# The place of three plain units in the first pair of each feed-forward stage, and of a set of constants

## The chip, the cores and the metric

The kernel runs on one core of a Trainium2 chip (trn2). The metric is device time of one execution in microseconds (us), the median of several runs. The engines named below are PE (matrix products), ACT (ScalarE), DVE (VectorE), POOL (GpSimd) and SP, which only issues transfers.

## The reference, cut to what matters

One decoder layer on 256 tokens of width 2048 in float32: a half-step feed-forward stage (width 5632), a mixer with two attention branches, and a second feed-forward stage, each with a residual and a layer norm. What the change touches:

```python
def _swiglu(x, w_gate, w_up, w_down):
    return (jax.nn.silu(x @ w_gate) * (x @ w_up)) @ w_down

# in the mixer, from the positions and four small vectors
cos, sin = jnp.cos(ang), jnp.sin(ang)
s = s - slopes[None, :, None, None, None] * dist[:, None, None, :, :]
s = jnp.where(_causal_mask(q0, q1), s, -jnp.inf)
lam = (jnp.exp(jnp.sum(lq1.astype(f32) * lk1.astype(f32)))
       - jnp.exp(jnp.sum(lq2.astype(f32) * lk2.astype(f32))) + lambda_init)
```

## The kernel before

**Products.** Every float32 factor is split in two parts: a rounded high part (L154, a cast on ACT) and the rest (L155, a subtraction on DVE). `triple` multiplies high by high, high by low and low by high: the three matmuls of L208, L209 and L210, 128x512 each. Split weights lie in a ring of pairs, `wring`; in gate and up there are six (`set_ring(6)`), so a weight block can be split only when the unit that used its pair last has run on PE. An even wring number is a pair's high part, the odd one behind it the low part.

**Units.** Work is queued in units. Each has a load (a DMA that SP issues), a `prep` (the split) and a `now` (its matmuls). `look(3, 4)` keeps three units loaded and four prepared ahead of the one that runs. Tile's scheduler then orders what each engine does, within the dependences and some `issue_after` constraints. Loads go out in SP's order: `raw` tiles of plain units (L482, 4 buffers, one is free when DVE has subtracted from it), and the seven-product blocks `sraw` and `eraw` (L443).

**The gate and up products** of a feed-forward stage work on pairs of column groups of the weights, w0 and w1. `Hybrid` computes most of the inner dimension by seven block products in place of eight (products 1 to 7), and the rest by plain units: `p` on w0, `q` on w1, 12 matmuls each. A product has three units: two with 6 matmuls, from `sraw` blocks of 128x1024, and a third with 3, from an `eraw` block of 128x512; 15 matmuls. The string in ORDERS gives the order; "n" stands where product 1 of the next pair goes. The key is (wide, seeded). All pairs of both feed-forward stages are wide; the first pair of each stage is not seeded (`p > 1` in the call), so (True, False) serves these two pairs alone. Feed-forward 1 runs from the start, feed-forward 2 behind the mixer; they are called stage 1 and stage 2 here.

**What the products read.** Product 1 uses block "11" of w0. When it has been split, a DMA on POOL that adds to its target (L458) puts block "12" of w1 on top of it; product 5 uses that sum. Product 3 uses block "22" as it is. For product 6, DVE adds the sum in "11" to "22" (L451); then POOL adds "12" to it by DMA (L453) for product 7. Products 1, 6 and 7 sum up in bank X, products 5 and 3 in bank Z, whose tile is called `tr`; the other banks' tiles are called `mm`. Behind product 5 ACT copies bank Z away (L409, in `after`), before product 3 writes it; behind products 1, 6 and 7 it copies bank X (L408).

**The constants of the mixer** (`setup`, L1099 to L1154: the mask, the biases of the attention, sines and cosines, lambda) are made during `down` of stage 1. `later(70, setup)` runs its code when 70 more units have run; from there on the scheduler places its instructions, most of them small ones on DVE.

Of the kernel before, what the change touches and what calls it, by code (L numbers as in the profile page):

```python
# [59 lines left out]
def layer_kernel(ctx: ExitStack, tc: tile.TileContext, a: dict, out: bass.AP):  # L60
# [42 lines left out]
    def later(n, fn):  # L103
        uid[0] += 1
        heapq.heappush(todo, (step[0] + n, uid[0], fn))
# [209 lines left out]
    class Extra:  # L315
# [7 lines left out]
        def make(self):  # L323
# [12 lines left out]
            for b, p in enumerate((2, 4)):  # L336
# [4 lines left out]
            V.scalar_tensor_tensor(out=lo, in0=a0, scalar=-1.0, in1=hi.bitcast(F32), op0=ALU.mult, op1=ALU.subtract)  # L341
            self.at_[1] = [hi, lo]

    ORDERS = {(False, False): "1pp5p36np27q4qqq", (True, False): "1p5p36np27q4qq",
              (False, True): "1pp5p36np27q4qqq", (True, True): "1p5p36np27q4qq"}
    WIDE = 5
    line = []
# [8 lines left out]
    class Hybrid:  # L356
# [35 lines left out]
        def group(self, w0, w1, done, wide=False, seeded=False, gates=False):  # L392
# [115 lines left out]
            else:  # L508
                order = ORDERS[wide, seeded]
            turn = {n: iter(range(WIDE if wide else 4, end + 1)) for n in range(2)}  # L510
# [421 lines left out]
    def ffn(n, x, wgu, wdn, residual, g, bt, each, first=None, between=None, nxt=None, cols=None, norm=None, pending=None):  # L932
# [100 lines left out]
                       ((24, 26, 48, 50) if pending is None else (13, 14, 60, 62), (94, 97, 100, 103)),  # L1033
                       35 if cols is None else None, pending, () if pending is None else (17, 32, 67, 82))
        if n == 1:
            later(70, setup)
        spare = []
        forms = {q: QuadForms(spare) for q in range(3)}
        down = Sliced(h_at)
# [462 lines left out]

    h1 = Acts(KD, "h1", (0, 1))
    ffn(1, xq, a["gu1"], a["dn1"], a["x"], a["ln1_g"], a["ln1_b"], keep(0), first_tokens, second_tokens, h1, a["ln1_cols"])

    yq = mixer(h1)
# [4 lines left out]
    for c in range(4):  # L1511
        project(a["w_out"][c], yq, KD, 512, lambda b, bank, c=c: ln.evac(c, b, bank),
                hook=at_unit(0, widen) if c == 3 else None)
    catch_up(0)

    ffn(2, h2, a["gu2"], a["dn2"], res[1], a["ln3_g"], a["ln3_b"],
        lambda b, c, z, o=slice(0, 512): (nc.scalar if o.start else nc.sync).dma_start(
            out[b * P:(b + 1) * P, c * 512 + o.start:c * 512 + o.stop], z), norm=ln,
# [66 lines left out]
def _build(arrays):  # L1585
    import numpy as np
    import concourse.bacc as bacc

    nc = bacc.Bacc("TRN2", target_bir_lowering=False, num_devices=1)
    aps = {k: nc.dram_tensor(f"in_{k}_dram", v.shape, mybir.dt.from_np(v.dtype), kind="ExternalInput").ap()  # L1590
           for k, v in arrays.items()}
    out = nc.dram_tensor("out_0_dram", (T, D), F32, kind="ExternalOutput").ap()
    with tile.TileContext(nc) as tc:
        layer_kernel(tc, aps, out)
    return nc
# [9 lines left out]
```

## Time and profile before

| | us |
|---|---|
| median of 3 runs | 1982.29 |
| lowest, highest run | 1978.77, 1983.79 |
| profiled execution, its own time | 1982.59 |
| its span | 1980.8 |
| PE busy in it | 1960.7 |
| mean granted clock of PE (1 is full) | 0.996 |

A row of the timeline gives start and duration in us, engine, line, operation, what is written and read, shapes, and in brackets how long the engine stood idle before it and what released it. Rows of POOLq and SPq are the issue of a transfer; its data lands later. A matmul's duration is the time through the array; a new one starts each 0.23 us. PE is idle where a start comes later than that.

### The profile page before, as it was taken

Reading aid. Unit: us, or ns where it says so; the run is one execution under the profiler, and the core shown is the slowest. Engines: PE = TensorE matmul, PEld = TensorE weight load, DVE = VectorE, ACT = ScalarE, POOL = GpSimd, SP = SyncE. Lnnn points to the kernel's source line nnn. Section 1 sums busy time; section 2 is a strip of 40 time slices with the busy share of each in tenths; the row PEclk is TensorE's granted clock in tenths of the full one; section 3 lists DMA queues with packets and bytes.
Section 4 is the critical chain, followed back from the end, with each engine's and each line's share of the span. In section 5 each row is a group of like instructions: output and inputs, shape, how many; then the busy total and the mean of one; then the engine's idle time right before and its main releaser. Section 6 shows DMA issues by size and latency. Waiting matters only on the chain. (4 is left out here: it accounts for less than half of the span.)

```text
span 1980.8 us, 25910 instructions
## 1 busy us (share of the span) xinstructions
PE 1960.7 (99%) x8751; PEld 1617.2 (82%) x8751; DVE 1743.7 (88%) x2161; ACT 1269.4 (64%) x1660; POOL 367.8 (19%) x600
## 2 busy tenths in 40 slices
PE   9899999999999999999999999999999999999998
PEld 8788888888878888888888888887888888888886
DVE  7799999999898879999987777779999999999997
ACT  6567766676656576666667655556767667766662
POOL 0112221222100010102241530011222123210000
PEclk9999999999999999999999999999999999999999
DMA  8888888787867657668686798688888878887773
GB/s 308 257 258 227 248 276 275 223 257 258 302 211 247 196 187 296 232 213 255 214 255 202 228 303 275 204 274 246 235 252 284 265 221 245 264 323 242 275 233 125
DMA packets 151958, 489.93 MB, mean 247 GB/s; under 512 B 21984, under 2 KB 22288, under 8 KB 151824
## 3 DMA queue, kind: packets, MB, share of 16 engines
q1 hardware_dynamic: 111744, 374.78, 53.4%
q0 software_dynamic: 39936, 113.35, 24.0%
q8 instruction: 68, 1.11, 0.2%
q14 instruction: 66, 0.54, 0.1%
q10 hardware_dynamic: 144, 0.13, 0.0%
HBM read 457.77 MB, written 30.41 MB: 246 GB/s over the span
## 5 line engine op out<-in xcount | busy, mean ns | idle before, releaser
L154 ACT CAST wring<-raw 128x1024 fp32r<-128x1024 f32 (+2 forms) x460 | 474.1, 1035 | 298.9 <-PE mm L210 211.7
L155 DVE TENSOR_TENSOR wring<-raw,wring 128x1024 fp32r<-128x1024 f32 (+2 forms) x460 | 545.4, 1198 | 111.0 <-ACT wring L154 108.7
L154 ACT CAST wring<-sraw 128x1024 fp32r<-128x1024 f32 x436 | 456.2, 1052 | 175.7 <-PE mm L210 67.4
L155 DVE TENSOR_TENSOR wring<-sraw,wring 128x1024 fp32r<-128x1024 f32 x436 | 524.5, 1217 | 47.8 <-ACT wring L154 43.7
L208 PE MATMUL mm<-wring,h 128*128 128x512 f32 (+2 forms) x1176 | 454.4, 386 | 0.0
L209 PE MATMUL mm<-wring,h 128*128 128x512 f32 (+2 forms) x1176 | 452.4, 385 | 0.4 <-DVE wring L155 0.4
L210 PE MATMUL mm<-wring,h 128*128 128x512 f32 (+2 forms) x1176 | 452.6, 385 | 0.0
L208 PEld LDWEIGHTS mm<-wring,h 128*128 128x128 f32 x1176 | 221.2, 188 | 47.0 <-ACT snap L409 3.3
L209 PEld LDWEIGHTS mm<-wring,h 128*128 128x128 f32 x1176 | 221.1, 188 | 44.1 <-DVE wring L155 1.1
L210 PEld LDWEIGHTS mm<-wring,h 128*128 128x128 f32 x1176 | 221.1, 188 | 43.8 <-DVE h L155 0.9
L209 PE MATMUL mm<-wring,xs 128*128 128x512 f32 x616 | 239.9, 390 | 0.2 <-DVE wring L155 0.2
L208 PE MATMUL mm<-wring,xs 128*128 128x512 f32 x616 | 240.1, 390 | 0.0
L210 PE MATMUL mm<-wring,xs 128*128 128x512 f32 x616 | 239.7, 389 | 0.0
L451 DVE TENSOR_TENSOR sraw<-sraw,sraw 128x1024 f32<-128x1024 f32 x128 | 153.7, 1217 | 1.2 <-DMA sraw<-in_wgm_dram 0.7
L209 PEld LDWEIGHTS mm<-wring,xs 128*128 128x128 f32 x616 | 115.7, 188 | 25.1 <-DVE wring L155 1.0
L210 PEld LDWEIGHTS mm<-wring,xs 128*128 128x128 f32 x616 | 115.6, 188 | 24.1
L208 PEld LDWEIGHTS mm<-wring,xs 128*128 128x128 f32 x616 | 115.6, 188 | 24.1
L749 POOL DMA_DIRECT2D hT<-blocks x176 | 98.4, 575 | 182.5 <-DVE blocks L747 94.8
L453 POOL DMA_DIRECT2D sraw<-in_gu_dram x40 | 35.1, 885 | 435.4 <-DVE sraw L451 410.5
L208 PE MATMUL mm<-wring,x 128*128 128x512 f32 x264 | 103.8, 396 | 0.4 <-ACT wring L154 0.4
L209 PE MATMUL mm<-wring,x 128*128 128x512 f32 x264 | 103.4, 392 | 0.2 <-DVE wring L155 0.2
L210 PE MATMUL mm<-wring,x 128*128 128x512 f32 x264 | 103.3, 391 | 0.0
(350 smaller groups left out, 2876.7 us busy)
## 6 DMA issues: line engine op xcount, KB each, us to landing
raw<-in_gu_dram SPq DMA_DIRECT2D x150, 512.0 KB, 6.3
raw<-in_dn_dram SPq DMA_DIRECT2D x140, 512.0 KB, 4.6
sraw<-in_gu_dram SPq DMA_DIRECT2D x120, 512.0 KB, 6.7
sraw<-in_gu_dram POOLq DMA_DIRECT2D x80, 512.0 KB, 7.0
sraw<-in_dn_dram SPq DMA_DIRECT2D x36, 512.0 KB, 5.7
raw<-in_w_out_dram SPq DMA_DIRECT2D x32, 512.0 KB, 4.4
eraw<-in_gu_dram SPq DMA_DIRECT2D x60, 256.0 KB, 6.9
hraw<-hT POOLq DMA_DIRECT2D x56, 256.0 KB, 5.1
```

The source lines that it names most:

```text
L154: cast[0] = S.copy(hi, src)
L155: lows[0] = V.tensor_tensor(out=lo, in0=src, in1=hi.bitcast(F32), op=ALU.subtract)
L208: PE.matmul(o, xh, wh, start=first, stop=False, skip_group_check=again)
L209: PE.matmul(o, xh, wl, start=False, stop=False, skip_group_check=again)
L210: PE.matmul(o, xl, wh, start=False, stop=last, skip_group_check=again)
L451: last = V.tensor_tensor(out=R[src][i], in0=R[src][i], in1=R[add[1]][i], op=ALU.add)
L453: nc.gpsimd.dma_start(R["22"][s], source("12", s), accum_op=ALU.add)
L749: nc.gpsimd.dma_start(to.rearrange("(g r) (i f) -> i r g f", g=4, i=4)[i], t[32 * i:32 * (i + 1), :].rearrange("r (g f) -> r g f", g=4))
```

## The change

```diff
--- before.py
+++ after.py
@@ -341,7 +341,7 @@
             V.scalar_tensor_tensor(out=lo, in0=a0, scalar=-1.0, in1=hi.bitcast(F32), op0=ALU.mult, op1=ALU.subtract)
             self.at_[1] = [hi, lo]
 
-    ORDERS = {(False, False): "1pp5p36np27q4qqq", (True, False): "1p5p36np27q4qq",
+    ORDERS = {(False, False): "1pp5p36np27q4qqq", (True, False): "1ppp536n27q4qq",
               (False, True): "1pp5p36np27q4qqq", (True, True): "1p5p36np27q4qq"}
     WIDE = 5
     line = []
@@ -1033,7 +1033,7 @@
                        ((24, 26, 48, 50) if pending is None else (13, 14, 60, 62), (94, 97, 100, 103)),
                        35 if cols is None else None, pending, () if pending is None else (17, 32, 67, 82))
         if n == 1:
-            later(70, setup)
+            later(84, setup)
         spare = []
         forms = {q: QuadForms(spare) for q in range(3)}
         down = Sliced(h_at)
```

The string keeps its three p, three q and all products. Before, one plain unit stood between products 1 and 5, one between 5 and 3, and one between the next pair's product 1 and product 2. In the new string all three stand between products 1 and 5: none between 5 and 3, and none between the next pair's product 1 and product 2. The second edit runs the code of `setup` 14 units later. Every engine has as many instructions as before.

Product 5 to product 3 on PE, stage 1. `xe` is the activations' side of a product's third unit, `xs` that of the first two, `x` that of a plain unit. Before, from the third unit of product 5 on:

```order
L208 MATMUL tr_546<-wring_120,xe_261 128x512
L209 MATMUL tr_546<-wring_121,xe_261 128x512
L210 MATMUL tr_546<-wring_120,xe_261 128x512
L208 MATMUL mm_530<-wring_118,x_215 128x512
L209 MATMUL mm_530<-wring_119,x_215 128x512
L210 MATMUL mm_530<-wring_118,x_216 128x512
```

After, the same third unit and what follows it:

```order
L208 MATMUL tr_576<-wring_116,xe_261 128x512
L209 MATMUL tr_576<-wring_117,xe_261 128x512
L210 MATMUL tr_576<-wring_116,xe_261 128x512
L208 MATMUL mm_497<-wring_120,xs_331 128x512
L208 MATMUL tr_576<-wring_114,xs_373 128x512
L209 MATMUL tr_576<-wring_115,xs_373 128x512
L210 MATMUL tr_576<-wring_114,xs_374 128x512
```

Before, a plain unit (`x`) follows product 5. After, the first matmul of product 6 (on `mm`) stands there, and behind it product 3 writes the bank that product 5 used.

The same stretch on ACT. Before, from the first cast of product 5 (`sraw_463`) to the copy of its bank; `sraw_465`, `sraw_466` and the second `eraw_471` are product 3's blocks:

```order
L154 CAST wring_104<-sraw_463 128x1024
L154 CAST wring_120<-eraw_471 128x512
L944 ACTIVATE sg_508<-mm_324 128x256
L154 CAST wring_102<-sraw_464 128x1024
L154 CAST wring_118<-raw_491 128x1024
L408 COPY snap_474<-mm_495 128x512
L154 CAST wring_116<-sraw_465 128x1024
L154 CAST wring_114<-sraw_466 128x1024
L154 CAST wring_104<-eraw_471 128x512
L409 COPY snap_474<-tr_546 128x512
```

After, from the first cast of product 5 to the copy of its bank:

```order
L154 CAST wring_120<-sraw_463 128x1024
L944 ACTIVATE sg_510<-mm_324 128x256
L154 CAST wring_102<-raw_488 128x1024
L154 CAST wring_118<-sraw_464 128x1024
L408 COPY snap_474<-mm_497 128x512
L154 CAST wring_116<-eraw_471 128x512
L154 CAST wring_114<-sraw_465 128x1024
L154 CAST wring_104<-sraw_466 128x1024
L154 CAST wring_102<-eraw_471 128x512
L154 CAST wring_120<-sraw_463 128x1024
L154 CAST wring_118<-sraw_464 128x1024
L409 COPY snap_474<-tr_576 128x512
```

Product 5's third block (the first `eraw_471`) is now cast behind its second (`sraw_464`), where it was ahead of it. Product 3's blocks take the ring pairs 114, 104 and 102, of which 104 and 102 were the second and third plain units' (`raw_483`, `raw_488`), and both casts of product 6 (`sraw_463` and `sraw_464` for the second time) stand ahead of the copy L409.

The loads that SP issues there. Before, from the plain unit ahead of product 3's blocks:

```order
L482 DMA raw_491<-in_gu_dram 128x1024
L443 DMA sraw_465<-in_gu_dram 128x1024
L443 DMA sraw_466<-in_gu_dram 128x1024
L443 DMA eraw_471<-in_gu_dram 128x512
L482 DMA raw_606<-in_gu_dram 128x1024
L482 DMA raw_677<-in_gu_dram 128x1024
L482 DMA raw_720<-in_gu_dram 128x1024
```

After, from the second plain unit on:

```order
L482 DMA raw_483<-in_gu_dram 128x1024
L482 DMA raw_488<-in_gu_dram 128x1024
L443 DMA sraw_465<-in_gu_dram 128x1024
L443 DMA eraw_471<-in_gu_dram 128x512
L482 DMA raw_684<-in_gu_dram 128x1024
L482 DMA raw_720<-in_gu_dram 128x1024
L482 DMA raw_731<-in_gu_dram 128x1024
L443 DMA sraw_466<-in_gu_dram 128x1024
```

Product 3's second block, `sraw_466`, is issued behind five plain loads in place of one, three of them behind its first block.

The mixer's constants on DVE, in `down` of stage 1. Before, in the middle of `setup`:

```order
L1134 TENSOR_SCALAR turns_4628<-turns_4628 128x128
L1144 TENSOR_TENSOR lp_4654<-lv_4652 128x256
L155 TENSOR_TENSOR wring_115<-raw_4497,wring_114 128x1024
L1136 SCALAR_TENSOR_TENSOR ang_4623<-turns_4628,ang_4623 128x128
L155 TENSOR_TENSOR wring_105<-sraw_3474,wring_104 128x1024
L1136 SCALAR_TENSOR_TENSOR ang_4623<-turns_4628,ang_4623 128x128
L1146 TENSOR_REDUCE ls_4656<-lp_4654 128x2
```

After, the rows at the same numbers:

```order
L1134 TENSOR_SCALAR turns_4832<-turns_4832 128x128
L1144 TENSOR_TENSOR lp_4858<-lv_4856 128x256
L155 TENSOR_TENSOR wring_115<-raw_4497,wring_114 128x1024
L155 TENSOR_TENSOR h_4782<-hraw_4699,h_4781 128x512
L155 TENSOR_TENSOR wring_105<-sraw_3474,wring_104 128x1024
L155 TENSOR_TENSOR h_4782<-hraw_4699,h_4781 128x512
L1136 SCALAR_TENSOR_TENSOR ang_4827<-turns_4832,ang_4827 128x128
```

The rows of `setup` up to here stand where they stood. From here on the L1136 rows come some places later; two subtractions of L155 for `h` go ahead.

## The prediction

> **What bounds the kernel now.** The page's busy times and the list of what PE waits for come first, then one undisturbed stretch by windows (columns: stretch, its length, busy time of PE, PEld, DVE, ACT and POOL, granted clock, DMA share, GB/s).
>
> ```profile
> PE 1960.7 (99%) x8751; PEld 1617.2 (82%) x8751; DVE 1743.7 (88%) x2161; ACT 1269.4 (64%) x1660; POOL 367.8 (19%) x600
> PE tr L208 <- ACT wring L154: 4.7, 2, 4.3
> PE tr L899 <- ACT pair L897: 4.1, 1, 4.1
> PE tr L209 <- DVE wring L155: 3.3, 3, 1.8
> 100.00:150.00 50.00, 50.00 (x221) 41.15 (x221) 46.45 (x55) 33.35 (x43) 9.56 (x14) 1.00 0.81 248
> ```
>
> PE is busy 99% of the span, and 221 matmuls fill 50 us: 0.226 us a step. No matmul goes or comes, so only the time in which PE stands still, or runs at a low clock, can change. The largest wait for a ring pair, 4.3 us on a `tr` tile, is product 5 of the first stage's first pair: where the diff works. Its PE rows (start, duration, what it waited for), from the last matmul of 5's first unit on, and the windows there:
>
> ```profile
> 57.72 0.39 PE L210 MATMUL tr<-wring,xs 128*128 128x512 f32 x1
> 62.38 0.51 PE L208 MATMUL tr<-wring,xs 128*128 128x512 f32 x1 [4.27 <-ACT wring L154]
> 63.64 0.79 PE L209 MATMUL tr<-wring,xs 128*128 128x512 f32 x1 [0.76 <-DVE wring L155]
> ...
> 69.78 0.43 PE L208 MATMUL mm<-wring,x 128*128 128x512 f32 x1
> 70.04 0.40 PE L209 MATMUL mm<-wring,x 128*128 128x512 f32 x1
> 62.40:69.80 7.40, 6.64 (x16) 4.97 (x17) 7.40 (x8) 4.74 (x7) 0.00 (x0) 0.54 0.34 117
> ```
>
> From 57.72 to 70.04 PE makes 17 steps, 3.85 us at 0.2267. They took 12.32: **8.47 us lost**. The clock row gives the shares: (1 − 0.54) × 7.40 = 3.4 us went to the low clock that followed, 5.1 to waiting. Why 5 was late, on ACT and POOL:
>
> ```profile
> 54.05 1.05 ACT L154 CAST wring<-sraw 128x1024 fp32r<-128x1024 f32 x1 [5.73 <-PE mm L210]
> 60.49 0.62 ACT L154 CAST wring<-eraw 128x512 fp32r<-128x512 f32 x1 [5.38 <-DMA eraw<-in_gu_dram]
> 61.29 1.03 ACT L154 CAST wring<-sraw 128x1024 fp32r<-128x1024 f32 x1
> 45.99 1.16 POOL L458 DMA_DIRECT2D eraw<-in_gu_dram  x1
> ```
>
> 5's third unit is cast at 60.49, when its accumulating DMA (issued at 45.99) has landed. 5's second unit stands behind it in ACT's order, so PE waited for a short tile that it needed last. Stage 2, the same place:
>
> ```profile
> 1339.99 0.39 PE L210 MATMUL tr<-wring,xs 128*128 128x512 f32 x1
> 1340.81 0.49 PE L208 MATMUL tr<-wring,xs 128*128 128x512 f32 x1 [0.43 <-ACT wring L154]
> 1342.06 0.50 PE L209 MATMUL tr<-wring,xs 128*128 128x512 f32 x1 [0.76 <-DVE wring L155]
> 1342.63 0.40 PE L208 MATMUL tr<-wring,xs 128*128 128x512 f32 x1
> 1339.98:1342.63 2.65, 1.46 (x5) 0.67 (x4) 2.14 (x4) 2.65 (x4) 0.00 (x0) 1.00 0.20 76
> 1350.13 0.39 PE L208 MATMUL mm<-wring,xs 128*128 128x512 f32 x1
> 1350.68 0.50 PE L209 MATMUL mm<-wring,xs 128*128 128x512 f32 x1 [0.17 <-DVE wring L155]
> ```
>
> 1339.99 to 1342.63 is 4 steps, 0.91 us, in 2.64: 1.74 us lost, at full clock. Product 6 starts 0.55 − 0.23 = 0.3 us late, and some 0.1 more in its next steps: 0.44.
>
> **What the change removes.** With three plains (12 matmuls, 2.72 us each) ahead of it, 5 starts 5.44 us later, at 62.0 instead of 56.6. Its second unit landed at about 57.8 (the second of the three accumulates) and now is cast ahead of the third unit, and the third is wanted only at 64.75 against a cast done near 61.1. All of 8.47 goes, in stage 2 all of 1.74 and, since 6 is delayed anyway, the 0.44. **−10.65 us.**
>
> **What it adds.** Nothing stands any more between 5 and 3 on PE. The plain that stood there gave the other engines 2.72 us for the copy of 5's bank (L409) and the splits of 3 and 6. Two things are now late, both in the orders shown above: one matmul of 6 stands ahead of 3 on PE, and ACT has L409, which must read bank Z before 3 writes it, behind 6's two casts. Durations, from the same chain in stage 2:
>
> ```profile
> 1343.98 0.62 ACT L154 CAST wring<-eraw 128x512 fp32r<-128x512 f32 x1
> 1345.94 0.68 DVE L155 TENSOR_TENSOR wring<-eraw,wring 128x512 fp32r<-128x512 f32 x1
> 1346.54 2.35 DVE L451 TENSOR_TENSOR sraw<-sraw,sraw 128x1024 f32<-128x1024 f32 x2
> 1347.84 2.14 ACT L154 CAST wring<-sraw 128x1024 fp32r<-128x1024 f32 x2 [2.75 <-DVE sraw L451]
> 1344.50 0.59 ACT L409 COPY snap<-tr 128x512 f32<-128x512 f32 x1
> ```
>
> 3's third unit takes the ring pair that the third plain frees (wring_102 in the rows of ACT), so its cast cannot start before 5 starts on PE; call that moment 0. Then: 0.2 + 0.62 the cast, 0.7 its low part, 1.2 the first add of L451, 1.1 the cast of 6: the single matmul of 6 runs at 3.9. With the steps by themselves, the add ends at 2.76; behind it follow both casts of 6 and the copy, 2.14 + 0.59: 3 may start at 5.5. 5's 15 matmuls end at 3.40 and the single one takes 0.23, so 3 should have started at 3.6: **1.9, with the restart 2.0 us lost**. This is the value for stage 2.
>
> In stage 1 the third unit of 5, which stands ahead of 3's casts in ACT's order, lands at 60.4 as before (I assume that the DMA queues are as full). 60.5 + 0.6 + 1.05 + 1.0 + 0.6: 3's casts end at 63.5; two more low parts on DVE and the add end at 66.2; 6's casts at 67.4 and 68.4, the copy at 69.0. 5 and the single matmul would have allowed 65.66: **3.1 to 3.3 us lost**; I take 3.1. If that DMA lands 1.5 us earlier, it is 2.0 as in stage 2.
>
> Does the clock drop? PE would stand from 65.4 to 67.4, then from 67.6 to 69.0. Rows of before, at the change's other place, with a similar gap:
>
> ```profile
> 589.76 0.51 PE L208 MATMUL tr<-wring,xs 128*128 128x512 f32 x1
> 592.09 0.80 PE L209 MATMUL tr<-wring,xs 128*128 128x512 f32 x1 [1.82 <-DVE wring L155]
> 589.31:595.82 6.51, 4.63 (x12) 3.17 (x11) 6.51 (x8) 3.51 (x5) 0.00 (x0) 0.74 0.64 196
> ```
>
> There 2.3 us between two starts were enough: (1 − 0.74) × 6.51 = 1.7 us lost to the clock. Stage 2's 1.74 us drew none (clock 1.00). The new gap in stage 1, 3.3 us with one matmul in it, is nearer to 590's: I add **1.7** for stage 1, nothing for stage 2; the bounds are 0 and the 3.4 of 62.40.
>
> [...]
>
> **The setup, 14 units later.** The order shows the same DVE rows in the same places up to row 612; only the short L1136 rows and what follows move by a few. The stall at 592.09 (DVE late with a low part) lies where DVE, still behind with the setup's work, is busy throughout:
>
> ```profile
> 565.55 1.02 DVE L1118 SCALAR_TENSOR_TENSOR bias<-dist,mask 128x384 f32<-128x384 f32 x2
> 572.83 1.02 DVE L1118 SCALAR_TENSOR_TENSOR bias<-dist,mask 128x384 f32<-128x384 f32 x2
> 595.36 0.22 DVE L1134 TENSOR_SCALAR turns<-turns 128x128 f32<-128x128 f32 x1
> ```
>
> The L1118 rows have not moved, so this edit costs nothing that I can see: **0**. Bounds: −4.0, if the stall went (2.3 us between starts and the clock's 1.7), and +0.4, if the setup ended late enough to hold up one more split (the 0.4 of the smallest waits on the list).
>
> **Sum.** 1982.59 (span 1980.8 and 1.8 around it) − 10.65 + 3.1 + 1.7 + 2.0 + 0 = **1978.7 us**. The profiled run lies 0.3 above the median of 1982.29, so I leave it. Measurements of this kernel can tell about 0.3% from no change, 5.9 us here: this gain of 0.2% counts as the same.
>
> **Rivals.**
> B, the same waits without a drop of the clock: 1977.0, or 1975.9 when the third unit also lands early. For it: the 1.74 us of stage 2 drew none. Against: 590 did.
> C, nothing takes the place of the stall, because the tile scheduler's order leaves more room than my chain: 1982.59 − 10.65 = 1971.9. Against: the ring pair of the third plain is a dependence, whatever the engines do.
> D, the setup does what a later place says, and the stall at 592 goes: 1978.7 − 4.0 = 1974.7. Against: the rows stand where they stood.
> E, **slower**: 3's second block (sraw_466 in SP's rows) is now issued behind three plain loads, and the last of them waits for a buffer. Loads there took:
>
> ```profile
> 39.93 7.96 SPq L482 DMA_DIRECT2D raw<-in_gu_dram  x3
> raw<-in_gu_dram SPq DMA_DIRECT2D x1, 512.0 KB, 9.7
> DMA to landing us min/median/max: 11.3/13.0/14.2
> ```
>
> The buffer is that of the second plain (raw_483), which lands 9.7 after 39.93, and is split 2.3 later: 51.9, so sraw_466 is issued near 52.2 instead of 48.5. With 7 us it lands at 59.2, hidden. With M its landing, the two splits, the add, 6's casts and the copy put 3 at M + 7.0: it decides from M = 62, and the gain is gone at about M = 64, 11.7 us after issue. The loads issued from 47.99 to 50.68 took 11.3 to 14.2. At 14.2, M = 66.4, 3 starts at 73.4, 7.7 late, with 3.4 for two slow windows: 1982.59 − 10.65 + 11.1 + 2.0 = **1985.0**. Against: those loads stood with six issued together and three accumulates; the load at 52.2 has fewer beside it.
>
> **How the numbers follow.** Forecast 0.50 (its own range 1977.8 to 1980.4: the low end with the wait at 2.2, the high end with a second slow window), B 0.28, C 0.07, D 0.06, E 0.09. The range leaves out C, the early end of D, and E beyond a small loss: 1974.3 to 1982.3. Faster by over 0.3% is below 1976.4: C, D and half of B, 0.26. Slower by over 0.3% is above 1988.2: the worst of E, 0.03. The same: 0.71.
>
> **What would show it.** In the changed kernel's profile: no wait of PE from 57.7 to 62; waits of about 2 and 1.4 us at the single matmul of 6 (for ACT's cast) and at 3's first (for L409), at about 65.4 and 67.6, and a lower clock behind them; some 2 us at the same two places in stage 2, at full clock; the wait near 590 as before. A wait of 3's second unit for its DMA means E; a stall at 590 that is gone means D. The forecast is wrong in its main step if the two new waits sum to under 1 us or over 5 in stage 1.

## The result and the profile after

| | before | after |
|---|---|---|
| median of 9 runs each, us | 1980.39 | 1976.14 |
| profiled execution, its own time | 1982.59 | 1975.02 |
| its span | 1980.8 | 1973.2 |

The ratio of after to before is 0.9974, with a 95% interval of 0.9964 to 0.9985. The forecast was 1978.7, no difference that this measurement tells from none (0.3%), in a range of 1974.3 to 1982.3. The measured gain of 0.26% is of that size, and the whole interval lies below 1. One of the nine runs after (2446.8 us, at a mean granted clock of 0.752) and one of the eight of the string-only kernel below (10628.98 us) were disturbed and are left out of the ratios.

Busy times of the changed kernel and, from the list of what its PE waits for, the three lines that bear on the change:

```profile
PE 1956.0 (99%) x8751; PEld 1614.6 (82%) x8751; DVE 1744.1 (88%) x2161; ACT 1269.9 (64%) x1660; POOL 367.7 (19%) x600
PE mm L208 <- ACT wring L154: 2.4, 1, 2.4
PE tr L208 <- ACT snap L409: 2.2, 2, 1.1
PE tr L209 <- DVE wring L155: 1.8, 1, 1.8
```

The wait of 4.3 us of a `tr` tile for its pair is gone. Two lines took its place: one that stood at 0.4 us before, and one for a copy (L409) that no matmul waited for before. PE in stage 1, timeline rows from the start of product 5 to product 3, then the window of the stretch behind 5:

```profile
62.22 0.39 PE L208 MATMUL tr<-wring,xs 128*128 128x512 f32 x1
...
65.40 0.39 PE L210 MATMUL tr<-wring,xe 128*128 128x512 f32 x1
68.17 0.51 PE L208 MATMUL mm<-wring,xs 128*128 128x512 f32 x1 [2.39 <-ACT wring L154]
69.81 0.50 PE L208 MATMUL tr<-wring,xs 128*128 128x512 f32 x1 [1.14 <-ACT snap L409]
70.15 0.39 PE L209 MATMUL tr<-wring,xs 128*128 128x512 f32 x1
```

```profile
65.40:70.10 4.70, 1.17 (x4) 0.47 (x3) 4.70 (x6) 2.91 (x4) 2.30 (x3) 1.00 0.39 98
```

Product 5 now runs through without a gap. Behind it come the two waits of the forecast, at the single matmul of 6 and at 3's first. From 65.40 to 70.15 PE makes three steps, 0.68 us, in 4.75: 4.1 us lost, against 8.47 before. The clock stayed at 1.00. The chain that set it, on ACT and DVE of the same run:

```profile
61.28 0.62 ACT L154 CAST wring<-eraw 128x512 fp32r<-128x512 f32 x1 [1.41 <-DMA eraw<-in_gu_dram]
61.81 2.00 ACT L154 CAST wring<-sraw 128x1024 fp32r<-128x1024 f32 x2
63.71 0.61 ACT L154 CAST wring<-eraw 128x512 fp32r<-128x512 f32 x1
67.07 2.20 ACT L154 CAST wring<-sraw 128x1024 fp32r<-128x1024 f32 x2 [2.75 <-DVE sraw L451]
69.18 0.58 ACT L409 COPY snap<-tr 128x512 f32<-128x512 f32 x1
```

```profile
65.17 0.68 DVE L155 TENSOR_TENSOR wring<-eraw,wring 128x512 fp32r<-128x512 f32 x1
65.77 2.35 DVE L451 TENSOR_TENSOR sraw<-sraw,sraw 128x1024 f32<-128x1024 f32 x2
```

It begins with product 5's third block at 61.28, goes through 3's three casts, DVE's low parts and the add, 6's two casts, and ends with the copy at 69.76. Product 3 starts 0.05 later. In stage 2, ACT and PE:

```profile
1337.46 0.62 ACT L154 CAST wring<-eraw 128x512 fp32r<-128x512 f32 x1 [0.98 <-PE mm L210]
1340.03 2.20 ACT L154 CAST wring<-sraw 128x1024 fp32r<-128x1024 f32 x2 [1.95 <-DVE sraw L451]
1342.14 0.58 ACT L409 COPY snap<-tr 128x512 f32<-128x512 f32 x1
```

```profile
1337.94 0.39 PE L208 MATMUL tr<-wring,xs 128*128 128x512 f32 x1
...
1341.11 0.40 PE L210 MATMUL tr<-wring,xe 128*128 128x512 f32 x1
1341.35 0.40 PE L208 MATMUL mm<-wring,xs 128*128 128x512 f32 x1
1342.78 0.50 PE L208 MATMUL tr<-wring,xs 128*128 128x512 f32 x1 [1.03 <-ACT snap L409]
1343.11 0.40 PE L209 MATMUL tr<-wring,xs 128*128 128x512 f32 x1
```

Only the second wait is there; from 1341.11 to 1343.11 PE lost 2.00 − 0.68 = 1.3 us, against 2.18 in this stage before. Third, the stall of stage 1's `down`, at 590 before:

```profile
585.00 0.50 PE L208 MATMUL tr<-wring,xs 128*128 128x512 f32 x1
587.32 0.50 PE L209 MATMUL tr<-wring,xs 128*128 128x512 f32 x1 [1.82 <-DVE wring L155]
584.54:591.05 6.51, 4.59 (x19) 3.30 (x18) 6.51 (x8) 3.51 (x5) 0.00 (x0) 1.00 0.63 198
```

The same wait, 1.82 us, but the clock behind it is 1.00 where it was 0.74. So of the 7.6 us between the two profiled executions, 4.4 went in stage 1, 0.9 in stage 2, some 1.7 is a slow clock that did not come this time, and the rest is in waits of about half a microsecond. The medians differ by 4.25; that they hold executions with and without the slow clock is an estimate from the mean granted clocks of the runs after, 0.996 to 0.998.

### The profile page after: what moved, and what is told of

Same layout as the page of the kernel before. It is cut to its first block, busy times and chain, and to the rows that moved or that the text cites. A ratio compares the mean times of both kernels' runs of the same rounds, so it can differ in the third digit from the quotient of the medians.

```text
span 1973.2 us, 25902 instructions
## 1 busy us (share of the span) xinstructions
PE 1956.0 (99%) x8751; PEld 1614.6 (82%) x8751; DVE 1744.1 (88%) x2161; ACT 1269.9 (64%) x1660; POOL 367.7 (19%) x600
## 5 line engine op out<-in xcount | busy, mean ns | idle before, releaser
L155 DVE TENSOR_TENSOR wring<-raw,wring 128x1024 fp32r<-128x1024 f32 (+2 forms) x460 | 544.9, 1197 | 111.4 <-ACT wring L154 109.3
L155 DVE TENSOR_TENSOR wring<-sraw,wring 128x1024 fp32r<-128x1024 f32 x436 | 524.2, 1216 | 41.6 <-ACT wring L154 37.4
L451 DVE TENSOR_TENSOR sraw<-sraw,sraw 128x1024 f32<-128x1024 f32 x128 | 153.6, 1216 | 1.4 <-DMA sraw<-in_wdk_dram 0.6
```

Of the source, the lines that this page charges most:

```text
L155: lows[0] = V.tensor_tensor(out=lo, in0=src, in1=hi.bitcast(F32), op=ALU.subtract)
L451: last = V.tensor_tensor(out=R[src][i], in0=R[src][i], in1=R[add[1]][i], op=ALU.add)
```

## The experiments

Theory: the gain is the string's alone, the stall of product 5 against the waits behind it; these come from the plain unit missing between 5 and 3. Rivals: the second edit gives a part; the waits have other causes.

### The two edits apart

```diff
-    ORDERS = {(False, False): "1pp5p36np27q4qqq", (True, False): "1p5p36np27q4qq",
+    ORDERS = {(False, False): "1pp5p36np27q4qqq", (True, False): "1ppp536n27q4qq",
```

> The new string, with setup where it was before. Theory (the whole gain comes from the string: the stall of product 5 in stage 1 and stage 2 goes, and shorter waits between 5 and 3 come): time as the changed kernel, ratio to before 0.997 to 0.998; PE waits of some 2.4 and 1.1 us behind product 5 in stage 1 and of 1.0 in stage 2, none ahead of it; the stall near 590 as before. Rival (part of the gain comes from the setup edit): ratio 0.9985 to 1.000.

Measured: 1976.42 against 1980.37 before, ratio 0.9976 (0.9965 to 0.9987). Its PE rows and the window behind:

```profile
65.95 0.50 PE L208 MATMUL mm<-wring,xs 128*128 128x512 f32 x1 [0.74 <-ACT wring L154]
67.59 0.50 PE L208 MATMUL tr<-wring,xs 128*128 128x512 f32 x1 [1.14 <-ACT snap L409]
65.00:72.00 7.00, 5.12 (x14) 3.68 (x14) 5.80 (x7) 3.99 (x5) 4.28 (x7) 0.76 0.94 202
```

The string alone gives the ratio of the change, within the intervals. The first wait is smaller here, 0.74 in place of 2.39: product 5's third block was cast at 59.06, not at 61.28. And here the clock did fall, to 0.76 of 7.00 us: 1.7 us, behind a shorter gap than the one that drew nothing above. This execution, of 1979.91 us, also lost 2.5 us at three waits from 546 to 555, ahead of setup's first row on DVE; the upper-half run below, with setup at 84, lost 1.1 there, and the changed kernel nothing.

```diff
-            later(70, setup)
+            later(84, setup)
```

> The old string, with setup 14 units later. Theory (the rows of setup stand where they stood, so it does nothing): ratio 0.999 to 1.001, product 5 stalls by over 4 us as before, the low part near 590 is late by 1.8 us as before. Rival (setup's place matters): ratio 0.998 or below, or the stall near 590 is gone or shorter by over 0.5 us.

Measured: 1979.75 against 1980.37, ratio 0.9997 (0.9988 to 1.0005). Product 5 waits (3.06 and 0.76 us, against 4.27 and 0.76 in the profile of before; that its third block landed later there is an estimate from these waits), and the other stall stands:

```profile
60.94 0.50 PE L208 MATMUL tr<-wring,xs 128*128 128x512 f32 x1 [3.06 <-ACT wring L154]
588.33 0.50 PE L209 MATMUL tr<-wring,xs 128*128 128x512 f32 x1 [1.82 <-DVE wring L155]
```

The second edit does nothing that can be measured here; the interval leaves room for 2.4 us of gain or 1.0 of loss. The expectation of "over 4 us" at product 5 was too narrow: in the profile of before that wait followed a transfer's landing (ACT cast the third block at 60.49, 5.38 us idle before it).

### A plain unit back between products 5 and 3

```diff
-(True, False): "1ppp536n27q4qq",
+(True, False): "1pp5p36n27q4qq",
```

> String 1pp5p36n27q4qq (two plain units ahead of product 5, one between 5 and 3), setup as in the changed kernel. Theory (the new waits come from the plain unit missing between 5 and 3): no wait at 6's first matmul and at 3's first in both stages; product 5 starts 2.7 us earlier and waits at most 0.5 us for its third unit; ratio to before 0.994 to 0.9955, some 4 to 6 us under the changed kernel. Rival (two plains are too few for the accumulating DMA of product 5): a wait of 1 to 3 us in product 5 of stage 1, ratio 0.996 to 0.998.

Measured: 1975.49, ratio 0.9972 (0.9961 to 0.9983): not told apart from the change, where 4 to 6 us less were expected, though both waits behind product 5 are gone in both stages, and 5 lost only 0.7 us in stage 1. What came instead stands at product 4, on PE in stages 1 and 2 (1.2 and 0.6 us lost), each time a wait for a split on DVE:

```profile
86.86 0.50 PE L209 MATMUL mm<-wring,xs 128*128 128x512 f32 x1 [0.95 <-DVE wring L155]
1359.48 0.50 PE L209 MATMUL mm<-wring,xs 128*128 128x512 f32 x1 [0.47 <-DVE wring L155]
```

In stage 1 DVE has no idle time from 71 to 89 us. A product unit with an add costs it 2.44 us (L451 and L155) against 1.36 of PE's six matmuls; a plain unit costs it 1.22 against 2.72. The theory was right on the cause of the waits and wrong on the time: the plain unit taken from in front of product 2 was missed at product 4, as the next run confirms.

### One more plain unit ahead of product 4

```diff
-(True, False): "1pp5p36n27q4qq",
+(True, False): "1pp5p36n27qq4q",
```

> String 1pp5p36n27qq4q: as the run e3_two_and_one, with one more plain unit of w1 ahead of product 4. Theory (a plain unit is cover: 2.7 us of PE against 1.2 us of DVE; with the third p ahead of product 5 nothing covered DVE's arrears at product 4, where e3 waited 1.2 us in stage 1 and 0.6 in stage 2): those two waits go, about 1.4 and 0.6 us, and nothing takes their place; 2 us under e3, ratio to before 0.995 to 0.9965. Rival (DVE's arrears only move on): waits of the same size at the next pair's product 5, ratio as e3, 0.997.

Measured: 1972.62 against 1980.16, ratio 0.9960 (0.9947 to 0.9972). No wait at product 4 in either stage, and none at the next pair. What is left in stage 1 is product 5 waiting at its first unit, 0.51 us for the cast and 0.76 for the low part; its third block holds up nothing. ACT casts 5's second block at 57.27, released by its transfer after 7.30 us idle, and the first only behind it, at 58.50. And the stall in `down` drew a slow clock this time (0.69 over 5.50 us, 1.7 us). ACT, then PE and the window of the stall:

```profile
57.27 1.05 ACT L154 CAST wring<-sraw 128x1024 fp32r<-128x1024 f32 x1 [7.30 <-DMA sraw<-in_gu_dram]
58.50 1.04 ACT L154 CAST wring<-sraw 128x1024 fp32r<-128x1024 f32 x1
60.85 0.50 PE L209 MATMUL tr<-wring,xs 128*128 128x512 f32 x1 [0.76 <-DVE wring L155]
584.50:590.00 5.50, 5.38 (x17) 4.29 (x18) 5.50 (x8) 1.63 (x2) 0.00 (x0) 0.69 0.88 243
```

### The chain behind product 5, taken apart

Two kernels are the changed kernel with one step of its chain altered. In the first, 3's third unit is split into the other half of its ring pair:

```diff
-                    pair = [v[:, :tiles * 512] for v in next_pair()]
+                    pair = [v[:, 512:] if tiles == 1 and p == 3 and wide and not seeded else v[:, :tiles * 512] for v in next_pair()]
```

> The changed kernel, but the third unit of product 3 in each stage's first pair is split into the upper half of its ring pair, not the lower. Theory (in stage 2 that cast began 0.48 us before product 5 because it writes only the lower half, which the third plain unit reads last three matmuls before its end): with the upper half the cast begins 0.2 us after product 5's first matmul, the wait ahead of product 3 in stage 2 grows from 1.2 us to 1.7 to 2.0, and 6's first matmul waits too (0.3 to 0.5); stage 1, set by the landing of product 5's third block, stays. Rival (that cast waits for its block's landing alone): stage 2 as it was, 1.2 us.

Measured: one execution, 1976.52. Its ACT and PE in stage 2, where product 5 starts at 1339.92:

```profile
1339.44 1.30 ACT L154 CAST wring<-eraw 128x512 fp32r<-128x512 f32 x2 [0.98 <-PE mm L210]
1342.70 1.05 ACT L154 CAST wring<-sraw 128x1024 fp32r<-128x1024 f32 x1 [1.95 <-DVE sraw L451]
1343.65 0.58 ACT L409 COPY snap<-tr 128x512 f32<-128x512 f32 x1
1344.13 1.05 ACT L154 CAST wring<-sraw 128x1024 fp32r<-128x1024 f32 x1
```

```profile
1343.80 0.49 PE L208 MATMUL mm<-wring,xs 128*128 128x512 f32 x1 [0.31 <-ACT wring L154]
1344.28 0.50 PE L208 MATMUL tr<-wring,xs 128*128 128x512 f32 x1
```

The first of the two casts at 1339.44 is that of another unit, which took the half that now was free early; 3's is the second, 0.2 us after 5's first matmul. Then 6's cast is at +2.78 and 6's matmul at +3.88, where the changed kernel had +2.09 and no wait: the half of the pair was worth 0.69 us, three matmuls. The expectation missed on product 3, though: its wait fell to 0.26. In this kernel the copy of L409 stands behind one of 6's casts, not behind both. The second kernel orders it so:

```diff
                     with tc.issue_after(last.ins) if last is not None and not small else nullcontext():
-                        split_in_line(not small, *pair, t)
+                        with tc.issue_after(copied[0].ins) if p == 6 and s == 1 and wide and not seeded else nullcontext():
+                            split_in_line(not small, *pair, t)
```

(`copied` holds the instruction of the copy.)

> The changed kernel, with the cast of product 6's second unit ordered behind the copy of product 5's bank (L409) on ACT, in each stage's first pair. Theory (3's first matmul waits for that copy, which stands behind both of 6's casts): the wait at 3's first matmul falls from 1.4 to about 0.3 us in stage 1 and from 1.2 to about 0.6 in stage 2, and the wait of 6's first matmul in stage 1 stays as its data land. Rival (3 waits for its own blocks there): no difference at 3.

Measured: one execution, 1971.64. ACT and PE in stage 1:

```profile
64.98 1.04 ACT L154 CAST wring<-sraw 128x1024 fp32r<-128x1024 f32 x1 [2.75 <-DVE sraw L451]
65.94 0.58 ACT L409 COPY snap<-tr 128x512 f32<-128x512 f32 x1
```

```profile
66.08 0.50 PE L208 MATMUL mm<-wring,xs 128*128 128x512 f32 x1 [1.00 <-ACT wring L154]
66.57 0.50 PE L208 MATMUL tr<-wring,xs 128*128 128x512 f32 x1
1339.44 0.50 PE L208 MATMUL tr<-wring,xs 128*128 128x512 f32 x1 [0.45 <-ACT snap L409]
```

Product 3 follows 6's matmul after 0.49 us in stage 1 (1.64 in the changed kernel); in stage 2 its wait is 0.45 (1.03). The second wait was the place of the copy in ACT's order, as the forecast had it.

### Where setup stands

The three kernels with one diff each here, and the two on POOL, have the string 1pp5p36n27qq4q.

```diff
-            later(84, setup)
+            later(110, setup)
```

> As e5_two_one_qq, with setup 110 units on in place of 84. In this kernel the rows of setup do move on DVE, by about a hundred places, behind the stall near 590. Theory (setup's DVE work is what makes the low part near 590 late): the wait of 1.8 us there is gone, and with it the slow clock that follows it in some runs: 2 to 4 us under e5. Rival (the wait has another cause there, or moves with setup): a wait of 1 to 2 us stays near 590 or comes near 690, time as e5.

Measured: 1970.89 against 1980.16, ratio 0.9951 (0.9938 to 0.9965), the best kernel of this study. Its runs went from 1969.69 to 1972.73, those with 84 from 1971.20 to 1974.51; the intervals overlap. The wait near 590 is gone, but others came where setup ended, some 2.8 us lost from 685 to 692, the largest in the layer norm:

```profile
687.03 1.50 PE L703 MATMUL tr<-ident,z 128*128 128x128 f32 x12 [1.20 <-DVE z L925]
```

Earlier, in a stretch where DVE had been 85% busy:

```diff
-            later(84, setup)
+            later(20, setup)
```

> As e5_two_one_qq, with setup 20 units on in place of 84: its rows stand some 60 places earlier on DVE, where DVE was busy 85% (495 to 540 us), not 98% (540 to 600). Theory (setup costs where DVE has no slack left before a split that PE waits for): the wait near 590 is gone and none comes near 690, 2 to 4 us under e5, 1 to 2 under e6; ratio to before 0.994 to 0.9955. Rival (setup's 6 us of DVE work come out as a PE wait wherever they stand): a wait of 1 to 2 us between 500 and 590, time as e5.

Measured: 1973.53 against 1981.60, ratio 0.9962 (0.9948 to 0.9975). The rival held: the wait near 590 is gone, and 3.7 us are lost where setup is now.

```profile
509.23 0.51 PE L209 MATMUL tr<-wring,xs 128*128 128x512 f32 x1 [1.57 <-DVE wring L155]
495.00:540.00 45.00, 42.05 (x182) 33.57 (x181) 42.66 (x74) 31.68 (x43) 9.11 (x17) 1.00 0.86 291
```

A mean of 85% over 45 us hid where the room was: with setup at 84, DVE was already busy for 19.93 of the 20 us from 500 to 520 (profile after; the splits and adds of a product), and the two longest of the new waits stand there. With three plains ahead of product 5, L409 ahead of 6's second cast, two q ahead of 4, and setup at 20 (the diff is to the changed kernel, beside that of the copy above):

```diff
-(True, False): "1ppp536n27q4qq",
+(True, False): "1ppp536n27qq4q",
...
-            later(84, setup)
+            later(20, setup)
```

> Three plain units ahead of product 5 as in the changed kernel, with L409 ahead of 6's second cast (as e7_copy_first), two q ahead of product 4 and setup 20 units on (as e8). Theory (each of these removes a wait of its own): waits behind product 5 of 1.4 to 3 us in stage 1 and 0.6 in stage 2, none at 590: time within 1.5 us of e8. Rival (the cover ahead of product 5 is worth more than that between 5 and 3): 2 us or more under e8.

Measured: 1974.05 against 1981.60, ratio 0.9966 (0.9953 to 0.9978), within 0.6 us of the run before. The waits behind product 5 were 0.5 us in stage 1 and 0.6 in stage 2; 2.6 us stood near 509. The mean granted clock of its profiled execution was 0.997, that of the run before 0.998.

Last, setup's arithmetic on POOL, each multiply-and-add in two instructions, one reduction left on DVE:

```diff
-            V.scalar_tensor_tensor(out=bias[h], in0=dist, scalar=-SLOPES[h], in1=mask,
-                                   op0=ALU.mult, op1=ALU.add)
+            GP.tensor_scalar(out=bias[h], in0=dist, scalar1=-SLOPES[h], scalar2=None, op0=ALU.mult)
+            GP.tensor_tensor(out=bias[h], in0=bias[h], in1=mask, op=ALU.add)
...
-        V.tensor_tensor(out=lp, in0=lv[:, 0:2, :], in1=lv[:, 2:4, :], op=ALU.mult)
+        GP.tensor_tensor(out=lp, in0=lv[:, 0:2, :], in1=lv[:, 2:4, :], op=ALU.mult)
```

> As e5_two_one_qq, with all of setup's arithmetic but one reduction on POOL in place of DVE (each multiply-and-add as two instructions). Theory (PE waits there because setup's rows stand among the splits on DVE): the waits near 590 are gone and none takes their place near 510 or 690; 2 to 4 us under e5 and under 1 above or 1 to 2 below e6, ratio to before 0.994 to 0.9955. Rival (POOL's work slows DVE, or holds up the transfers that POOL issues): the splits near 570 take longer than 1.22 us, or PE waits for a block that POOL fetched; time as e5 or above.

Measured: 1996.90 against 1980.32, ratio 1.0081 (1.0068 to 1.0095). DVE came to its one reduction and stood 20 us behind POOL's chain; PE waited 18.7:

```profile
586.22 0.42 DVE L1148 TENSOR_REDUCE ls<-lp 128x2 f32<-128x256 f32 x1 [20.14 <-POOL lp L1146]
```

The same with the block of lambda first, and on DVE:

```diff
     def setup():
+        lv = tmp_tile([P, 4, P], "lv")
...
+        V.tensor_tensor(out=lp, in0=lv[:, 0:2, :], in1=lv[:, 2:4, :], op=ALU.mult)
...
         GP.memset(mask, 0.0)
```

> As e10_setup_on_pool, with the block of lambda and the scaled gains first in setup and on DVE, so that DVE never waits for POOL in setup. Theory (the 20 us in which DVE stood in e10 were its one reduction waiting behind POOL's chain): that wait is gone; near 590 no wait over 0.5 us; between e6 and e5, ratio to before 0.9945 to 0.996. Rival (POOL's arithmetic slows DVE beside it: splits took 1.4 to 1.5 us there in e10, not 1.2): splits of 1.4 us or more between 550 and 590 and PE waits of 1 to 3 us there, ratio 0.996 to 0.998.

Measured: 1992.84 against 1981.80, ratio 1.0063 (1.0049 to 1.0077). Now ACT stood, at the sine, behind the same chain, with the splits queued behind it; PE waited 17.2. ACT and DVE:

```profile
592.18 0.31 ACT L1155 ACTIVATE sincos<-ang 128x128 f32<-128x128 f32 x1 [24.66 <-POOL ang L1154]
```

```profile
562.65 2.04 DVE L155 TENSOR_TENSOR wring<-sraw,wring 128x1024 fp32r<-128x1024 f32 x1
593.45 1.23 DVE L155 TENSOR_TENSOR wring<-raw,wring 128x1024 fp32r<-128x1024 f32 x1 [19.56 <-ACT wring L154]
```

Neither run tells whether the wait near 590 needs setup on DVE, since 17 us of standing still come before it; both had it, after the stall, at 608 and 606. That stays open; that the wait goes when setup stands elsewhere, the runs with 110 and with 20 show.

## Why the prediction was right, and where it was not

**What the change removes: right.** Product 5 started at 62.22 (forecast 62.0) and ran through; −10.65 us was the size of both stalls and of the delay at 6 in that execution. The stall was larger there than in others: the setup-only run shows 3.06 where the profile of before has 4.27, so part of the 8.47 was that execution's own, its later landing by the estimate above. With two slow stretches of the clock besides (3.4 us lost around product 5, 1.7 behind 590), that execution stands 2.2 us over before's median of nine.

**The new waits: right in place and cause, off in size both ways.** In stage 2 the step that failed is "its cast cannot start before 5 starts on PE": I took the ring pair as freed by the third plain's last matmul. The cast writes only half of the pair, which was read last three matmuls earlier, so the chain began at −0.48 in place of +0.2, and 1.3 us were lost where I had 2.0. The upper-half run shows the forecast's chain to the tenth (3.88 against 3.9). In stage 1 I had product 5's third block "as before"; its cast came 0.8 later, and 4.1 us were lost for 3.1. In the string-only run it came 1.4 earlier than forecast, and 2.3 were lost. One term of the sum hangs on a landing that varies by 2 us (the cast that it released began at 58.85 in the run with three plains, L409 first, qq and setup at 20, at 60.30 in the upper-half run and at 61.28 in the profile after); the forecast should have carried it as a range.

**The clock: a chance, not a size.** I added 1.7 in stage 1, by the likeness of the gap to that at 590, and gave the case without it 0.28. The profile after had rival B's clock with a longer wait. The string-only run had the drop (0.76 over 7.00 us, 1.7 us) behind 2.3 us lost in waits, and the upper-half run (steps of 0.43 us in place of 0.23) behind a wait of 2.15. So both cases are one order of work in different executions. Counted from before's median of nine, the forecast is 1976.5 and rival B 1974.8; the median of 1976.14 lies between.

**Setup: right.** Its rows stood where they had stood, and the ratio is 0.9997.

**The slower rival: close.** 3's second block was issued at 52.26 (forecast 52.2) and landed after this:

```profile
sraw<-in_gu_dram SPq DMA_DIRECT2D x1, 512.0 KB, 9.4
```

That is some 61.7, against 62.0 from which it would have decided by the forecast's chain. Its cast began at 62.76, behind that of the first block and without a wait.

**The sum** of 1978.7 was 2.6 us over the median, since the profile it started from lies 2.2 over its own median of nine runs. That the change of the sum, −3.9, came within 0.4 of the medians' −4.25 is in part luck: the waits of the profile were 1.0 longer in stage 1 and 0.7 shorter in stage 2, the clock's 1.7 behind product 5 did not come there, and the −10.65 holds 3.4 of slow clock, of which the other execution of the old string (setup only) had half.

(One slip in the description ahead of the prediction: the copy of bank X behind product 7 is on line 409 too, not 408. Nothing rests on it.)

## What to carry to other kernels

Units of work that cost the busiest engine more than its helper are cover, and cover can be spent once: ask of each place that such a unit leaves what stood behind it, not only what it hides where it goes. A wait that follows a transfer's landing belongs in a sum as a range over executions, not as the value of one profile. Before work is moved to an idle engine, look for every engine whose order of work holds an instruction that reads its results: here one small instruction stood before the splits behind it for 20.14 us on DVE, in the other run for 24.66 on ACT.

## What the runs showed of the hardware

The same stall drew a slow clock in some executions and not in others: the wait of 1.82 us in `down` (1.83 in the string-only run) stands in the profiles of before, after and six of the experiments (string only, setup only, two and one, upper half, the first with qq, copy first), and the clock fell behind it in three of the eight: before (0.74 over 6.51 us), the one with qq (0.69 over 5.50), and string only, where PE's steps from 590.64 to 593.63 took 0.42 to 0.43 us in place of 0.23. That is 1.6 to 1.7 us each time. In the profile after the clock was 1.00 over 6.51 us there, in the setup-only run 1.00 over 5.50, and the steps behind the wait took 0.22 to 0.24 us from the second on in the other three. Around product 5 of stage 1 it was no different: in before it was 0.54 over 7.40 us (3.4 us lost), in the setup-only run 0.74 over 6.60 us (1.7), in the string-only run 0.76 over 7.00 behind 2.3 us lost in waits; in the upper-half run the steps behind the wait of 2.15 took 0.42 to 0.43 us from 69.48 on; and in the profile after, where 4.1 us were lost, it was 1.00 from 65.40 to 80.00.

What decides whether the clock falls is not shown. The length of the wait alone does not tell these executions apart: the same wait was followed by a drop in three and by none in five, and the 4.1 us of the profile after by none.

In the run with POOL at setup's arithmetic and lambda on DVE, DVE's split of 128x1024 took up to 2.04 us (at 562.65, while that arithmetic was under way), and 1.23 at 593.45, behind the sine that waited for the last of it.
